# A two-layer attention trunk: four modulation rows, the first loads, the first norm, the rotary tables and the steps of the last two heads are put elsewhere

## The chip, the cores and the metric

The kernel runs on one core of a Trainium2 chip. The metric is the device time of one execution in microseconds; lower is better. A core has a matrix engine (TensorE, PE in the profile), a vector engine (VectorE, DVE), a scalar engine (ScalarE, ACT), a small general engine (GpSimd, POOL) and a queue engine (SyncE, SP) that issues nearly all of this kernel's DMAs. Each engine runs its own instructions in a fixed order; between engines there are semaphores. TensorE writes its sums to PSUM banks, from which VectorE and ScalarE read.

## The reference

One sequence of 256 tokens and 2048 features passes through two layers. Layer 0 mixes tokens by NSA attention (16 query heads, 4 key and value heads, a compressed, a selected and a window branch), layer 1 by differential attention (8 heads, each with two softmaxes). Each mixer is followed by an MLP of 8192 hidden features with squared ReLU. Every sub-layer is modulated by shift, scale and gate vectors that are computed from one vector c. All data are float32.

```python
mod_all = einsum('bd,lde->lbe', silu(c), ada_w) + ada_b[:, None, :]   # ada_w (2, 2048, 6*2048)
for i in range(2):
    sh1, sc1, g1, sh2, sc2, g2 = jnp.split(mod_all[i][:, None, :], 6, axis=-1)
    h = rms_norm(x, attn_norm_g[i]) * (1.0 + sc1) + sh1
    y = nsa_mixer(h, positions, ...) if i == 0 else diff_mixer(h, positions, ...)
    x = x + g1 * y
    h = rms_norm(x, mlp_norm_g[i]) * (1.0 + sc2) + sh2
    x = x + g2 * (jnp.square(jax.nn.relu(h @ w1)) @ w2)
# diff_mixer, per head: a = softmax(q0 k0) - lam * softmax(q1 k1); o = rms_norm(a @ v) ; y = o @ w_out
```

## The kernel before

x stays in SBUF with features on partitions: `xT` is 128 x 16 x 256, 16 blocks (kt) of 128 features by 256 tokens. Weights arrive as `raw` tiles of 128 x 1024 (512 KB). For most matrix products ScalarE rounds such a tile to `wH`, VectorE forms `wL = raw - wH` (`split`, L254 on), and TensorE does three products for every one of the reference: wH by the rounded activations, wH by their rest, wL by the rounded ones. There are 721 such tiles.

**The modulation.** `ada_w` is read as 192 rows of 128 x 2048 (1 MB each). A row is multiplied by silu(c) and summed on VectorE by one `scalar_tensor_tensor` (stt). The 32 rows of layer 0's first scale and shift are called `adarow` and belong to the first stage, two per block (`lead_ada`, L720). The other 160, `adaraw`, come from a queue (`ada_step`): each tile of weights adds a rate to a credit, and each full credit takes a row. The rates are the constants RA, RB, RC for NSA, DR for the projections of layer 1, MR0, MR1 and CR for the MLPs. Four rows of this queue (40 to 43, `PE_ROWS`) are stored otherwise and summed by TensorE: `pe_row` makes 16 small matmuls into `adps` for each, `pe_add` four more into `ade`.

**The first stage.** It begins with the first norm (L431 to L436): ScalarE squares each block of xT, TensorE sums the squares over partitions with a matrix of ones into `nps`, and `rstd_of` takes the root in VectorE and ScalarE steps named `nst`, `ny`, `nu`. Then come 16 blocks kt. Each needs its two rows, one weight tile for the compressed branch (16 matmuls `psc`) and one for values or keys (8 matmuls `psv` or `psk`). h of a block is made by VectorE (`nt`), ScalarE (`h`, twice) and VectorE (`h`, the rest). Blocks 0 to 7 use psc and psv, then psk is done for them, and blocks 8 to 15 use psc and psk. `trig` and `rope_table` (L440 on) make sines, cosines and the rotary tables from the positions; the code calls them in block kt = 3. The compression weights `cwk`, `cwv` follow the window projection `psw`.

**The heads of layer 1.** Four groups g of two heads. Per group `dk`, `dq` and `dv` are projections in four steps u. Work for the heads waits in a list `pend`: normalising and turning keys and queries (`norm`, `both`, `flip`; transposes `tps` of `qr`), then for each of two heads `scores` (`dsc`), `turn` (`aps`), `pv` (`dops`, then `on`, a normalised copy) and `back` (`otp`, then `od`). `pop()` takes the first entry of the list at each step u of a later projection; what is left at the end of dv of group 3 is taken in `dwo`, the output projection, one entry per step.

**What sets the order.** A scheduler of the tile framework orders the instructions of every engine by priority; the text of the program gives the priority, `high_priority` moves a row ahead, and `issue_after(ins)` places an instruction behind `ins` on that engine without making it wait. Tile pools limit how far ahead loads go: 5 buffers for raw, 3 for `adaraw`, 8 in the pool of `adarow` of which h holds four, 3 each for wH and wL, and in PSUM banks 4 for projections, 1 in `sd` and 3 in `sc`.

Of the kernel before, what the change touches and what calls it, by code (L numbers as in the profile page):

```python
# [19 lines left out]
P = 128  # L20
# [16 lines left out]
RA, RB, RC = 1.34, (1.25, 1.5, 1.5, 1.5), (2.0, 0.9)  # L37

PE_ROWS = range(40, 44)
DR = 0.4  # L40
MR0 = 0.72
# [36 lines left out]
def emit(ctx, tc, nc, a):  # L78
# [45 lines left out]
    for q in range(4):  # L124
        nc.sync.dma_start(xT[:, q * 4:(q + 1) * 4, :], a["xT"][:, q * 4:(q + 1) * 4, :])
# [28 lines left out]
    last_load = [None]  # L154

# [5 lines left out]


    e4 = cst.tile([P, 1], F32, name="e4")
    V.tensor_reduce(out=e4, in_=ident[:, 0:P:32], axis=mybir.AxisListType.X, op=ALU.add)
    pe_rows, pe_open, pe_sums = [], [], []

    def on_pe(l, vec, kt):
        return l == 0 and ada_q.index((l, vec, kt)) in PE_ROWS

    def pe_row(l, vec, kt, r):  # L170
        w = r.rearrange("p (k n) -> p k n", k=KT)
        if not pe_open:
            pe_open.append(sc("adps"))
        ps = pe_open[0]
        j = len(pe_open) - 1
# [4 lines left out]
        pe_open.append(kt)  # L180
        if j == 3:
            four = sm.tile([P, 4, P], F32, tag="qr", bufs=QRB, name="four")
            act(four, ps.rearrange("p (j n) -> p j n", j=4))
            pe_sums.append((l, vec, kt - 3, four))
            pe_open.clear()

    def pe_add():
        while pe_sums:
            l, vec, kt, four = pe_sums.pop(0)
            ps = sd("ade")  # L190
            for j in range(4):
                TE.matmul(ps[:, j:j + 1], four[:, j], e4, start=j == 0, stop=j == 3)
            e = vec * KT + kt
            tt(mod[:, l, vec, kt:kt + 4], ps[:, :4], bT[:, l, e:e + 4], ALU.add)

    def pe_flush(keep):
        if len(pe_rows) > keep:
            pe_add()
            for _ in range(2):
                pe_row(*pe_rows.pop(0))  # L200

    def ada_tile(l, vec, kt):
# [3 lines left out]
        if on_pe(l, vec, kt):  # L206
            pe_rows.append((l, vec, kt, r))
            pe_flush(2)
            return
# [4 lines left out]
    def ada_row(vec, kt):  # L214
        r = actp.tile([P, D], F32, tag="act", name="adarow")
        nc.sync.dma_start(r, a["adaT"][0, vec * KT + kt])
        acc = acc_tile(0, vec)[:, kt:kt + 1]
        stt(r, r, 1.0, cbc, ALU.mult, ALU.mult, accum_out=acc)
        return acc

    def ada_vec(l, vec):
        e = vec * KT
        cuts = [0] + [kt for kt in range(1, KT) if on_pe(l, vec, kt) != on_pe(l, vec, kt - 1)] + [KT]
        for lo, hi in zip(cuts, cuts[1:]):
            if not on_pe(l, vec, lo):
                tt(mod[:, l, vec, lo:hi], acc_tile(l, vec)[:, lo:hi], bT[:, l, e + lo:e + hi], ALU.add)
# [21 lines left out]
    def ada_until(l, vec):  # L248
# [3 lines left out]
        if any(p[:2] == (l, vec) for p in pe_rows + pe_sums):  # L252
            while pe_rows:
                pe_flush(0)  # L254
            pe_add()
# [982 lines left out]
```

## Time and profile before

| | us |
|---|---|
| three timed runs | 2356.14, 2358.07, 2363.26 |
| their median | 2358.07 |
| the profiled execution | 2358.31 |
| its span in the trace | 2356.3 |
| TensorE busy | 2323.1 (99%) |
| VectorE busy | 1734.8 (74%) |
| ScalarE busy | 1183.5 (50%) |

The profile shows one execution. A row of a timeline gives the start, the time from the first instruction's start to the last one's end, and, in brackets, how long the engine had been idle before and what released it. Matmuls are pipelined, so the lengths of two rows overlap; the distance between starts is what a row costs. PEclk is the clock that was granted to TensorE: 1.00 is 2.4 GHz, 0.5 is 1.2 GHz, and a value between them for a stretch is a mean over time at either. In 40 equal slices of the span TensorE stands at 9 tenths busy or more in all but the first, the granted clock at 9 or more in all but the first, and the share of the DMA engines is 9 tenths in the first four.

### The profile page before, as it was taken

The numbers are of one execution on the slowest core, as the hardware profiler recorded it, in microseconds if no ns is written. First come the engines' busy times: TensorE is split into PE (matmuls) and PEld (weight loads), VectorE is DVE, ScalarE is ACT, GpSimd is POOL, SyncE is SP. The second block draws the span as 40 slices with busy tenths as digits, with TensorE's granted clock in tenths as the row PEclk, the third lists the DMA queues.
The fourth block names the chain that finished last, engine by engine and source line by source line (L and its number), as shares of the span: only waits on it lengthen the run. The fifth ranks groups of instructions, "written<-read, shape, count | busy, mean of one in ns | idle before, by whom it ended". The sixth has DMA issues, their size and how long they took to land.

```text
span 2356.3 us, 34910 instructions
## 1 busy us (share of the span) xinstructions
PE 2323.1 (99%) x13465; PEld 1998.3 (85%) x13465; DVE 1734.8 (74%) x2418; ACT 1183.5 (50%) x2055; POOL 44.8 (2%) x41
## 2 busy tenths in 40 slices
PE   7999999999999999999999999999999999999999
PEld 5767778998888888888898888799988888888888
DVE  6867999699888888888888777766755555555555
ACT  3223788455345345445556556555643543543553
POOL 0000000000000000000000100000000000000000
PEclk8999999999999999999999999999999999999999
DMA  9999777779888888888867666645555555555554
GB/s 358 404 371 354 292 306 264 267 279 371 337 308 324 329 310 327 319 308 333 306 226 247 222 238 233 210 159 170 194 188 187 183 189 187 187 188 187 187 194 147
DMA packets 139846, 612.19 MB, mean 260 GB/s; under 512 B 15648, under 2 KB 16288, under 8 KB 114080
## 3 DMA queue, kind: packets, MB, share of 16 engines
q1 hardware_dynamic: 139536, 609.71, 71.6%
q8 instruction: 105, 1.72, 0.3%
q14 instruction: 61, 0.50, 0.1%
q10 hardware_dynamic: 144, 0.26, 0.0%
HBM read 607.81 MB, written 2.10 MB: 259 GB/s over the span
## 4 chain that ended last, share of the span: by engine, by line
PE 71%; DVE 1%; DMA 1%; issue 1%; ACT 0%; POOL 0%; POOLq 0%; SPq 0%; DVEq 0%
PE m L301 36%; PE m L308 17%; PE dwo L293 1%; PE dwo L294 1%; PE dwo L295 1%; PE m L304 1%; PE dk L285 1%; PE dk L286 1%; PE dk L287 1%; PE dv L287 1%; PE dv L286 1%; PE dv L285 1%; PE dq L285 1%; PE dq L286 1%; PE dq L287 1%; DMA adaraw<-adaT 1%
## 5 line engine op out<-in xcount | busy, mean ns | idle before, releaser
L97 ACT ACTIVATE wH<-raw 128x1024 fp32r<-128x1024 f32 x721 | 762.3, 1059 | 895.7 <-PE m L301 655.2
L262 DVE TENSOR_TENSOR wL<-raw,wH 128x1024 fp32r<-128x1024 f32 x721 | 877.5, 1222 | 451.0 <-ACT wH L97 449.5
L301 PE MATMUL m<-hd,wH 128*128 128x512 f32 x2048 | 710.4, 396 | 0.0
L301 PE MATMUL m<-hn,wH 128*128 128x512 f32 x1792 | 624.7, 397 | 0.0
L308 PE MATMUL m<-hd,wL 128*128 128x256 f32 x1920 | 534.5, 280 | 4.5 <-DVE wL L262 4.5
L308 PE MATMUL m<-hn,wL 128*128 128x256 f32 x1680 | 470.7, 281 | 0.0
L301 PEld LDWEIGHTS m<-hd,wH 128*128 128x128 f32 x2048 | 376.1, 188 | 80.2
L301 PEld LDWEIGHTS m<-hn,wH 128*128 128x128 f32 x1792 | 329.7, 188 | 71.0
L103 DVE SCALAR_TENSOR_TENSOR adaraw<-adaraw,cbc 128x2048 f32<-128x2048 f32 x156 | 356.2, 2285 | 25.0 <-DMA adaraw<-adaT 23.2
L308 PEld LDWEIGHTS m<-hd,wL 128*128 128x128 f32 x1920 | 361.4, 189 | 12.7 <-DVE wL L262 6.1
L308 PEld LDWEIGHTS m<-hn,wL 128*128 128x128 f32 x1680 | 317.2, 189 | 5.9 <-DVE wL L262 0.2
L103 DVE SCALAR_TENSOR_TENSOR xT<-m,mod,xT 128x256 f32<-128x256 f32 x256 | 108.8, 478 | 38.8 <-PE m L301 38.7
L103 DVE SCALAR_TENSOR_TENSOR adarow<-adarow,cbc 128x2048 f32<-128x2048 f32 x32 | 73.2, 2286 | 8.7 <-DMA adarow<-adaT 4.4
L293 PE MATMUL dwo<-od,wH 128*128 128x256 f32 x256 | 73.5, 290 | 0.6 <-ACT od L97 0.6
L295 PE MATMUL nwo<-o,wL 128*128 128x256 f32 x256 | 73.3, 286 | 0.0
L295 PE MATMUL dwo<-od,wL 128*128 128x256 f32 x256 | 73.0, 286 | 0.0
L293 PE MATMUL nwo<-o,wH 128*128 128x256 f32 x256 | 73.0, 285 | 0.0
L294 PE MATMUL dwo<-od,wH 128*128 128x256 f32 x256 | 72.9, 285 | 0.0
L294 PE MATMUL nwo<-o,wH 128*128 128x256 f32 x256 | 72.8, 284 | 0.0
L293 PE MATMUL m_z<-z,wH 128*128 128x258 f32 x256 | 72.7, 284 | 0.0
L735 PEld LDWEIGHTS psc<-h,raw 128*128 128x128 f32 x256 | 51.7, 205 | 24.5 <-ACT h L97 10.3
L294 PE MATMUL m_z<-z,wH 128*128 128x258 f32 x256 | 72.3, 283 | 0.0
(317 smaller groups left out, 3242.8 us busy)
## 6 DMA issues: line engine op xcount, KB each, us to landing
raw<-w SPq DMA_DIRECT2D x512, 512.0 KB, 4.3
adaraw<-adaT SPq DMA_DIRECT2D x160, 1024.0 KB, 7.0
raw<-di SPq DMA_DIRECT2D x96, 512.0 KB, 4.1
adarow<-adaT SPq DMA_DIRECT2D x32, 1024.0 KB, 12.4
raw<-ws SPq DMA_DIRECT2D x48, 512.0 KB, 10.5
raw<-wi SPq DMA_DIRECT2D x32, 512.0 KB, 6.4
raw<-nwo SPq DMA_DIRECT2D x32, 512.0 KB, 5.0
raw<-dwo SPq DMA_DIRECT2D x32, 512.0 KB, 3.5
```

Of the source, the lines that this page charges most:

```text
L97: return S.activation(out=out, in_=in_, func=func, **kw)
L103: V.scalar_tensor_tensor(out, in0, scalar, in1, op0=op0, op1=op1, **kw)
L262: last_split[1] = V.tensor_tensor(out=L[:, :n], in0=raw[:, :n], in1=H[:, :n].bitcast(F32), op=ALU.subtract).ins
L285: TE.matmul(ps, xh, H[:, off:off + n], start=first, stop=False)
L286: TE.matmul(ps, xh, L[:, off:off + n], start=False, stop=False)
L287: TE.matmul(ps, xl, H[:, off:off + n], start=False, stop=last)
L293: TE.matmul(ps, H[:, off:off + m], xh, start=first, stop=False)
L294: TE.matmul(ps, H[:, off:off + m], xl, start=False, stop=False)
L295: TE.matmul(ps, L[:, off:off + m], xh, start=False, stop=last)
L301: big = lambda stop: TE.matmul(ps.rearrange("p (a t) -> p a t", a=2), H[:, off:off + P], at, start=first, stop=stop)
L308: TE.matmul(ps[:, :T], L[:, off:off + P], at[:, 0], start=False, stop=False)
L735: TE.matmul(ps_c[i][n // 2][:, (n % 2) * T:(n % 2 + 1) * T], w[:, i * 512 + n * P:i * 512 + (n + 1) * P], full, start=f and n % 2 == 0, st ...
```

## The change

- The four rows on TensorE go: `pe_row`, `pe_add` and `pe_flush` are removed, and all 160 rows are summed by VectorE.
- The rates of the row queue become RC (2.2, 0.8), DR 0.45, MR0 0.65.
- The first norm squares four blocks per instruction: ScalarE squares 128 x 1024, VectorE another 128 x 1024, VectorE adds the two, and TensorE sums 4 blocks for each half instead of 8.
- The loads of the first stage get a fixed order behind the last load of xT; the weight tiles of a block come behind its rows, `posi`, `rowb` and `mk` behind a weight tile.
- `trig`, the tables and the casts of masks come behind the rows of the fourth block.
- Three of the four value weights of the compression (`cwv`) are loaded in blocks 13 to 15, ahead of `cwk`.
- In dv of group 3 two entries of `pend` are taken at each of the four steps, in an order in which the two heads go side by side.

```diff
-RA, RB, RC = 1.34, (1.25, 1.5, 1.5, 1.5), (2.0, 0.9)
-
-PE_ROWS = range(40, 44)
-DR = 0.4
-MR0 = 0.72
+RA, RB, RC = 1.34, (1.25, 1.5, 1.5, 1.5), (2.2, 0.8)
+DR = 0.45
+MR0 = 0.65
...
-    def pe_row(l, vec, kt, r):
...
-        for k in range(KT):
-            i = k % 4
-            TE.matmul(ps[i * 32:(i + 1) * 32, j * P:(j + 1) * P], cs[:, k:k + 1].to_broadcast([P, 32]), w[:, k],
-                      start=j == 0 and k < 4, stop=j == 3 and k >= KT - 4, tile_position=(0, i * 32))
...
     def ada_row(vec, kt):
         r = actp.tile([P, D], F32, tag="act", name="adarow")
-        nc.sync.dma_start(r, a["adaT"][0, vec * KT + kt])
+        with tc.issue_after(last_load[0]) if vec * KT + kt in FIRST else nullcontext():
+            last_row[0] = nc.sync.dma_start(r, a["adaT"][0, vec * KT + kt]).ins
         acc = acc_tile(0, vec)[:, kt:kt + 1]
-        stt(r, r, 1.0, cbc, ALU.mult, ALU.mult, accum_out=acc)
+        last_row[1] = V.scalar_tensor_tensor(r, r, 1.0, cbc, op0=ALU.mult, op1=ALU.mult, accum_out=acc).ins
         return acc
+
+    last_row = [None, None]
+    FIRST = [v * KT + kt for v in range(2) for kt in range(KT // 2)]
...
-    for kt in range(KT):
-        sq = sm.tile([P, T], F32, tag="nsq", name="nsq0", bufs=4)
-        act(sq, xT[:, kt, :], AF.Square)
-        TE.matmul(nps[:, :T], ones, sq, start=(kt == 0), stop=(kt == KT - 1))
+    for i in range(2):
+        two = [p.tile([P, 1024], F32R, tag=tag, name="sq0").bitcast(F32) for p, tag in ((whp, "wh"), (wlp, "wl"))]
+        for j in range(2):
+            x4 = xT[:, (i * 2 + j) * 4:(i * 2 + j + 1) * 4, :].rearrange("p k t -> p (k t)")
+            if j:
+                tt(two[j], x4, x4, ALU.mult)
+            else:
+                act(two[j], x4, AF.Square)
+        tt(two[0], two[0], two[1], ALU.add)
+        for k in range(4):
+            TE.matmul(nps[:, :T], ones, two[0][:, k * T:(k + 1) * T], start=i + k == 0, stop=i * 4 + k == 7)
...
+    def pop_two(u):
+        pend.pop(0)()
+        pend.pop(1 if u == 0 else 0)()
...
-        wc = wcols(kt, 0)
-        wv = wcols(kt, 1)
+        with tc.issue_after(last_row[0]):
+            wc = wcols(kt, 0)
+            wv = wcols(kt, 1)
...
         if kt == 3:
-            trig()
-            tab_ks = rope_table(ROW_KS, 0, 2, "tab_ks")
...
+            with tc.issue_after(last_row[1]):
+                trig()
+                tab_ks = rope_table(ROW_KS, 0, 2, "tab_ks")
...
+        if kt >= KT - 3:
+            cwv.append(values_weights(kt - KT + 3))
...
-            ps = xs_group(f"dv{g}_", lambda u: a["di"][g * 3, u], h1, DR, lambda u: pop(g == 3 and u < 2))
+            ps = xs_group(f"dv{g}_", lambda u: a["di"][g * 3, u], h1, DR, lambda u: pop_two(u) if g == 3 else pop())
```

Three places of the resulting order are shown. The first is VectorE in the first stage; `trb` is the angle of `trig`, `adarow` a row of a block, and `h_202`, `h_203` hold h of blocks 0 to 3 and 4 to 7 (`h_170`, `h_171` after). Before, from the end of block 0's h to the second row of block 1:

```order
21 L100 TENSOR_TENSOR h_202<-h_237,h_202 128x256
22 L445 CAST trb<-posi 128x3
23 L107 TENSOR_SCALAR trb<-co,trb 128x64 x3
24 L109 TENSOR_SCALAR trb<-trb 128x192
25 L107 TENSOR_SCALAR trb<-trb 128x192
26 L109 TENSOR_SCALAR trb<-trb 128x192 x2
27 L100 TENSOR_TENSOR trb<-trb 128x192
28 L103 SCALAR_TENSOR_TENSOR trb<-trb 128x192 x6
29 L109 TENSOR_SCALAR trb<-trb 128x192
30 L103 SCALAR_TENSOR_TENSOR adarow,adaacc<-adarow,cbc 128x2048
31 L107 TENSOR_SCALAR trs<-trs 128x3x64
32 L103 SCALAR_TENSOR_TENSOR Amod<-adaacc,b_211,smallT 128x1
```

After, from the second row of block 3 to the first row of block 4; block 1 now has only its rows and its own steps on VectorE:

```order
42 L400 CAST trb<-posi 128x3
43 L736 CAST maskb<-mk 128x288
44 L98 TENSOR_TENSOR mod<-adaacc,smallT 128x1
45 L105 TENSOR_SCALAR trb<-co,trb 128x64 x3
46 L737 CAST identb<-co 128x128
47 L107 TENSOR_SCALAR trb<-trb 128x192
48 L105 TENSOR_SCALAR trb<-trb 128x192
49 L98 TENSOR_TENSOR h_170<-h_299,h_170 128x256
50 L107 TENSOR_SCALAR trb<-trb 128x192 x2
51 L98 TENSOR_TENSOR trb<-trb 128x192
52 L101 SCALAR_TENSOR_TENSOR trb<-trb 128x192 x5
53 L170 SCALAR_TENSOR_TENSOR adarow,adaacc<-adarow,cbc 128x2048
```

The angles and tables have moved from between blocks 0 and 1 to between blocks 3 and 4.

The second is ScalarE at the end of the heads, where `dwo` runs on TensorE. Before, with `on` the normalised result of a head and `od` its turned copy:

```order
815 L97 ACTIVATE wH<-raw 128x1024 x6
816 L97 ACTIVATE on,dss<-dops 128x256 x2
817 L97 ACTIVATE on<-dops,dss 128x256 x2
818 L97 ACTIVATE wH<-raw 128x1024 x2
819 L97 ACTIVATE on,dss<-dops 128x256 x2
820 L97 ACTIVATE on<-dops,dss 128x256 x2
821 L97 ACTIVATE od_13952<-otp,subg 128x256
822 L97 ACTIVATE z_1_0_14196<-mod 128x4x2
823 L97 ACTIVATE od_13952<-otp,subg 128x256 x3
824 L97 ACTIVATE wH<-raw 128x1024
```

After:

```order
807 L95 ACTIVATE wH<-raw 128x1024 x6
808 L95 ACTIVATE on,dss<-dops 128x256 x2
809 L95 ACTIVATE on<-dops,dss 128x256 x2
810 L95 ACTIVATE wH<-raw 128x1024 x2
811 L95 ACTIVATE on,dss<-dops 128x256 x2
812 L95 ACTIVATE on<-dops,dss 128x256 x2
813 L95 ACTIVATE wH<-raw 128x1024 x2
814 L95 ACTIVATE od_13832<-otp,subg 128x256
815 L95 ACTIVATE z_1_0_14143<-mod 128x4x2
816 L95 ACTIVATE od_13832<-otp,subg 128x256
817 L95 ACTIVATE wH<-raw 128x1024 x2
818 L95 ACTIVATE od_13832<-otp,subg 128x256 x2
```

Behind the second head's `on` now stand two weight tiles before the first `od`, and before there were none; the four `od` of the last pair of heads all stand behind them.

The third is VectorE in the first MLP, where `hd` is the hidden layer and `xT` takes up the result. Before:

```order
622 L100 TENSOR_TENSOR hd_0_3_5002<-sq,hd_0_3_5002 128x2x256
623 L262 TENSOR_TENSOR wL<-raw,wH 128x1024
624 L100 TENSOR_TENSOR hd_0_3_5002<-sq,hd_0_3_5002 128x2x256
625 L262 TENSOR_TENSOR wL<-raw,wH 128x1024
626 L103 SCALAR_TENSOR_TENSOR adaraw,adaacc<-adaraw,cbc 128x2048 x2
627 L262 TENSOR_TENSOR wL<-raw,wH 128x1024 x2
628 L103 SCALAR_TENSOR_TENSOR adaraw,adaacc<-adaraw,cbc 128x2048
629 L262 TENSOR_TENSOR wL<-raw,wH 128x1024 x2
```

After, at the same weight tiles (the 117th and on):

```order
628 L210 TENSOR_TENSOR wL<-raw,wH 128x1024
629 L101 SCALAR_TENSOR_TENSOR adaraw,adaacc<-adaraw,cbc 128x2048
630 L98 TENSOR_TENSOR hd_0_3_4900<-sq,hd_0_3_4900 128x2x256 x2
631 L210 TENSOR_TENSOR wL<-raw,wH 128x1024 x2
632 L101 SCALAR_TENSOR_TENSOR adaraw,adaacc<-adaraw,cbc 128x2048
633 L210 TENSOR_TENSOR wL<-raw,wH 128x1024 x2
634 L101 SCALAR_TENSOR_TENSOR adaraw,adaacc<-adaraw,cbc 128x2048
635 L210 TENSOR_TENSOR wL<-raw,wH 128x1024 x2
```

Two rows in a run have become single rows with two weight tiles between them.

## Rows read from the trace of the kernel before

**Rows 1.** The page, part 1: span, busy time and instructions of each engine

```profile
span 2356.3 us, 34910 instructions
...
PE 2323.1 (99%) x13465; PEld 1998.3 (85%) x13465; DVE 1734.8 (74%) x2418; ACT 1183.5 (50%) x2055; POOL 44.8 (2%) x41
```

**Rows 2.** Waits of PE, whole span: line, releaser, total, times, longest (us)

```profile
PE psc L735 <- ACT h L97: 7.1, 2, 4.3
...
PE m L308 <- DVE wL L262: 4.5, 3, 1.7
PE otp L1073 <- ACT on L97: 3.4, 2, 2.8
PE tps L532 <- DVE qr L100: 3.0, 2, 2.0
```

**Rows 3.** The page, part 5: costliest groups; mean ns behind the busy time

```profile
L262 DVE TENSOR_TENSOR wL<-raw,wH 128x1024 fp32r<-128x1024 f32 x721 | 877.5, 1222 | 451.0 <-ACT wH L97 449.5
...
L103 DVE SCALAR_TENSOR_TENSOR adaraw<-adaraw,cbc 128x2048 f32<-128x2048 f32 x156 | 356.2, 2285 | 25.0 <-DMA adaraw<-adaT 23.2
```

**Rows 4.** Timeline of PE around 450 and 484 us: start, length, instructions

```profile
449.49 1.95 PE L178 MATMUL adps<-adaraw,cs 128*32 128x128 f32 x64
451.38 0.39 PE L293 MATMUL nwo<-o,wH 128*128 128x256 f32 x1
...
483.73 1.05 PE L192 MATMUL ade<-e,four 128*128 128x1 f32 x8
484.65 0.37 PE L293 MATMUL m_z<-z,wH 128*128 128x258 f32 x1
```

**Rows 5.** Busy time per stretch (x instructions), PEclk, DMA share, GB/s

```profile
400.00:485.00 85.00, 84.92 (x790) 83.07 (x789) 62.39 (x109) 47.34 (x91) 0.00 (x0) 1.00 0.71 260
500.00:540.00 40.00, 40.00 (x310) 38.60 (x309) 39.96 (x66) 28.82 (x54) 0.00 (x0) 1.00 0.71 258
...
1480.00:1520.00 40.00, 36.41 (x167) 29.08 (x166) 26.85 (x37) 20.19 (x46) 3.37 (x4) 1.00 0.60 212
1560.00:1580.00 20.00, 16.59 (x110) 15.85 (x110) 9.83 (x19) 9.68 (x21) 0.69 (x1) 0.83 0.25 82
```

**Rows 6.** Timeline of DVE, first MLP

```profile
584.45 2.29 DVE L103 SCALAR_TENSOR_TENSOR adaraw<-adaraw,cbc 128x2048 f32<-128x2048 f32 x1
...
586.66 2.29 DVE L103 SCALAR_TENSOR_TENSOR adaraw<-adaraw,cbc 128x2048 f32<-128x2048 f32 x1
```

**Rows 7.** Timeline of PE: idle time before an instruction, and its releaser

```profile
590.15 0.74 PE L308 MATMUL m<-hd,wL 128*128 128x256 f32 x4 [1.08 <-DVE wL L262]
...
1498.66 0.63 PE L532 MATMUL tps<-co,qr 128*128 128x128 f32 x4 [2.00 <-DVE qr L100]
...
1565.68 0.66 PE L1073 MATMUL otp<-co,on 128*128 128x128 f32 x4 [2.84 <-ACT on L97]
1566.90 1.22 PE L293 MATMUL dwo<-od,wH 128*128 128x256 f32 x4 [0.56 <-ACT od L97]
```

**Rows 8.** Timeline of PE in the first stage

```profile
22.18 5.98 PE L735 MATMUL psc<-h,raw 128*128 128x256 f32 x16 [4.28 <-ACT h L97]
...
34.41 6.69 PE L735 MATMUL psc<-h,raw 128*128 128x256 f32 x16 [2.82 <-ACT h L97]
...
51.25 3.62 PE L735 MATMUL psc<-h,raw 128*128 128x256 f32 x16
...
58.14 3.62 PE L735 MATMUL psc<-h,raw 128*128 128x256 f32 x16
```

**Rows 9.** Timeline of DVE in the first stage

```profile
22.60 0.43 DVE L100 TENSOR_TENSOR h<-h,h 128x256 fp32r<-128x256 f32 x1 [1.02 <-ACT h L97]
...
27.74 2.28 DVE L103 SCALAR_TENSOR_TENSOR adarow<-adarow,cbc 128x2048 f32<-128x2048 f32 x1
...
34.87 0.42 DVE L100 TENSOR_TENSOR h<-h,h 128x256 fp32r<-128x256 f32 x1
...
50.04 2.29 DVE L103 SCALAR_TENSOR_TENSOR adarow<-adarow,cbc 128x2048 f32<-128x2048 f32 x1 [0.97 <-DMA adarow<-adaT]
```

More of the change, by code (lines that the diff above doesn't have):

```diff
@@ L1 @@
 import math
-from contextlib import ExitStack, contextmanager
+from contextlib import ExitStack, contextmanager, nullcontext
 import numpy as np
@@ L159, in acc_tile @@
         return adaacc[l, vec]
[L163 to L168, printed above, removed]
-    def pe_row(l, vec, kt, r):
[L171 to L175, printed above, removed]
-        for k in range(KT):
-            i = k % 4
-            TE.matmul(ps[i * 32:(i + 1) * 32, j * P:(j + 1) * P], cs[:, k:k + 1].to_broadcast([P, 32]), w[:, k],
-                      start=j == 0 and k < 4, stop=j == 3 and k >= KT - 4, tile_position=(0, i * 32))
[L180 to L200, printed above, removed]
     def ada_tile(l, vec, kt):
@@ L251, in ada_until @@
             ada_step(1.0)
[L252 to L255, printed above, removed]
     def split(raw, n=1024):
@@ L730, in full_of, with values_weights @@
         return modulate_full(h, kt, rstd, Amod[:, 0, 0, kt:kt + 1], mod[:, 0, 0, kt:kt + 1])
+    def values_weights(lu):
+        wv = adap.tile([P, 8, 256], F32, tag="ada", name="cwv")
+        with tc.issue_after(last_load[0]):
+            nc.sync.dma_start(wv.rearrange("p l f -> p (l f)"), a["cw1"][1, lu])
+        return wv
+    cwv = []
     def c_mm(w, full, f, la):
@@ L756, in emit @@
         if kt == 1:
-            nc.sync.dma_start(posi, a["posT"])
-            nc.sync.dma_start(rowb, a["rows"][:, :ROW_LAM * DH].to_broadcast([P, ROW_LAM * DH]))
             mk = wkp.tile([P, 288], F32, tag="qT", name="mk", bufs=1)
-            nc.sync.dma_start(mk, a["consts"][:, CO_M0:CO_N])
+            with tc.issue_after(last_load[0]):
+                nc.sync.dma_start(posi, a["posT"])
+                nc.sync.dma_start(rowb, a["rows"][:, :ROW_LAM * DH].to_broadcast([P, ROW_LAM * DH]))
+                nc.sync.dma_start(mk, a["consts"][:, CO_M0:CO_N])
         if kt == 3:
-            trig()
-            tab_ks = rope_table(ROW_KS, 0, 2, "tab_ks")
-            tab_kw = rope_table(ROW_KW, 0, 2, "tab_kw")
-            V.tensor_copy(maskb, mk)
-            V.tensor_copy(identb, ident)
-            w2c = wkp.tile([P, 2, 2, DH], F32, tag="qT", name="w2c", bufs=1)
-            nc.sync.dma_start(w2c, a["cw2"])
+            with tc.issue_after(last_row[1]):
+                trig()
+                tab_ks = rope_table(ROW_KS, 0, 2, "tab_ks")
+                tab_kw = rope_table(ROW_KW, 0, 2, "tab_kw")
+                V.tensor_copy(maskb, mk)
+                V.tensor_copy(identb, ident)
+                w2c = wkp.tile([P, 2, 2, DH], F32, tag="qT", name="w2c", bufs=1)
+                nc.sync.dma_start(w2c, a["cw2"])
     for i in range(2):
@@ L825, in cmp_part @@
         nc.sync.dma_start(wk.rearrange("p l f -> p (l f)"), a["cw1"][0, lu])
-        wv = adap.tile([P, 8, 256], F32, tag="ada", name="cwv")
-        nc.sync.dma_start(wv.rearrange("p l f -> p (l f)"), a["cw1"][1, lu])
+        wv = cwv.pop(0) if cwv else values_weights(lu)
         for j in range(8):
@@ L1193 @@
     ins["adaT"] = c_(ada_w.transpose(0, 2, 1).reshape(DEPTH, NVEC, P, D))
-    for n in PE_ROWS:
-        e = (2, 4, 3, 5)[n // KT] * KT + n % KT
-        ins["adaT"][0, e] = ada_w[0][:, e * P:(e + 1) * P].reshape(KT, P, P).transpose(1, 0, 2).reshape(P, D)
     wi = nsa_w_in[0]
```

12 lines of the change are left out of this document (2 added, 10 removed).

## The prediction

> **What bounds the kernel now.** I read the page's busy times first. TensorE is busy 2323.1 of 2356.3 us [rows 1], so 33.2 us at most can be won by taking waits away; more has to come from its own work. The waits of TensorE come next [rows 2]: four kinds make 18.0 of the 33.2 us. They lie in three places, and the change touches all three: the first stage (7.1 us for h), single weight tiles `wL` (4.5), and the heads of layer 1 (3.4 for `on`, 3.0 for `qr`). Last I read the stretches [rows 5]: VectorE is full in 500 to 540 us (39.96 of 40), yet TensorE has no idle time there; a row too early in a run, as at 590 us, does cost 1.08 [rows 7]. The granted clock is 1.00 in all of them but the last, 1560 to 1580, where it is 0.83, a mix of the levels 2.4 and 1.2 GHz. So a time is set here by TensorE's work, by a late VectorE or ScalarE result at few places, and by the clock after such a wait.
>
> **The four rows on TensorE.** One group of 64 small matmuls costs 1.89 us (from 449.49 to the next work at 451.38), and there are two; the eight matmuls of `ade` cost 0.92 (483.73 to 484.65) and about 0.2 in front of them [rows 4]. All of it is in TensorE's own line: 2 x 1.89 + 1.1 = **-4.9 us**. VectorE gets four rows more, 4 x 2.285 = 9.1 us [rows 3], and by the rates six rows more (43 to 49) stand before the end of the NSA output projection: 6 x 2.285 = 13.7 us. In 400 to 485 us VectorE is idle 85 - 62.4 = 22.6 us [rows 5], which covers them. Not all of that is free when it is wanted: the last NSA heads' steps then stand behind a row. Bounds: nothing, and a row's rest with a wL behind, 1.5; I take +0.7. Without the cover the price is up to 9.1, which is a rival below.
>
> **The first MLP.** TensorE waits 1.08 us at 590.15 because the wL it needs stands behind two rows in a run, at 584.45 and 586.66 [rows 6, 7]. In the new order single rows alternate there with two weight tiles, since rows are ahead by four. Of the three waits for wL (4.5 us, the longest 1.7 [rows 2]) this one goes. A second of 1.7 near 1147 us stands behind a row and a burst of xT steps; the lower rate moves the row away, and it goes too, nearly. The third, in front of which only xT steps stand, stays. So 1.08 + 1.7 = 2.8, of which I take **-2.7**; bounds 0 (another tile becomes late; a run of two rows now stands at the 113th tile) and -4. That the rates leave as many rows to layer 1 costs nothing in the second half: VectorE has room (in 1480 to 1520 us it is busy 26.8 of 40 [rows 5]).
>
> **The paired heads.** Today the two heads of the last group follow each other and their ends have no work beside them. The list of waits gives 3.0 (qr) and 3.4 (on), and 0.56 for od at 1566.90 [rows 2, 7]. After the 2.84 us at 1565.68 the granted clock falls: a mean of 0.83 over 20 us [rows 5] is 3.4 us of time lost at 1.2 GHz. Together 10.4; about 1.5 more is lost as the array runs empty and fills at each of five waits (an estimate of 0.3 each), so some 11.9 us are there to win. The new order takes two steps per weight pair in dv, so `norm` and `flip` of the queries come where dv still runs, and after the last `on` ScalarE does two weight tiles, while TensorE has 48 matmuls of dwo in front of the first `otp`; at 84.9 / 790 = 0.107 us each [rows 5] that is 5.2 us for a chain that needed 2.84 more than it had. What is late next: two heads' scores need four score banks in a row where three exist, and the fourth waits until ScalarE has done one exponential behind a weight tile: its `wL` sibling takes 1.22 us [rows 3], so I take 1.3; and 0.3 for the single `sd` bank. Sum -11.9 + 1.6 = **-10.3**. Bounds: -12 if nothing new waits; -6 if both heads' softmax pushes three weight tiles late by 1.22 us each and the idle time at the end is only halved.
>
> **The first stage.** Block 0 starts at 22.18 now, block 1 after 2.82 us of waiting at 34.41 [rows 8]. The wide squares leave ScalarE and TensorE earlier, but block 0's two rows must still land and pass VectorE, so I leave 22.18 as it is (bounds 0.7 either way). Then the angles: today they stand between block 0's h (22.60) and block 1's second row (27.74, the first of that block on VectorE), 4.8 us, and the tables follow until 34.87 [rows 9]. Without them blocks 1 to 3 come earlier; the 2.82 us and the second stretch at 1.2 GHz go (6.69 against 3.62 us for the same 16 matmuls, 3.07 [rows 8]). Together that is 5.9 us. But it isn't kept. The rows of a block come by DMA, and block 4's first row already waits for its DMA, 0.97 us at 50.04 [rows 9]. The angles now stand around exactly this block's rows: some 5 us of them in front of the first row, the rest and the tables, 2.5 us, in front of h. Block 4 then starts at about 50.04 + two rows of 2.2 + 2.5 for angles and tables + 1 for its own small steps = 57.9, against 58.14 [rows 8], and TensorE, done with block 3 5.9 us earlier than now, at about 52.2, waits some 5.7 us in front of it. A wait of 2.82 was followed by the lower clock [rows 8], so this one will be as well: block 4 loses up to 3.07 that it doesn't lose today, of which I count 2 from its later start to the keys of blocks 0 to 7. The loads that wait for freed buffers behind it shift, but three of today's short waits for them go. **+0.9** remains; bounds -4 (the angles fit into VectorE's wait for block 4's row) and +3 (all of the lower clock is kept, and the shift too). The masks and `w2c` moved with it cost VectorE 0.5 us inside the same wait.
>
> TensorE's clock is where a page speaks against this move. The row shows that 16 matmuls of a block take 6.69 us behind an idle time of 2.82, and 3.62 at full clock [rows 8]; and that a wait of 2.00 us at 1498.66 was followed by none of it (granted clock 1.00 in 1480 to 1520 [rows 5, 7]). The Trainium skill, "TensorE: Matmul & The Clock Gate", section "Why this matters for your kernels", advises against idle gaps between bursts of matmuls, since the engine goes back to half clock after them. By that rule one gap of 5.7 us before block 4 is no better than the present gap before block 1; without the rule the sum would be some 2 us lower.
>
> **Window keys and compression weights.** In front of the first wL of `psw` VectorE now copies all of `kcT`. That stage has no wait in the list today; at worst two weight tiles are late by 1.22 us each [rows 3]. I take +1.3 (0 to 2.5). The three early `cwv` loads fall into a stretch with DMA to spare and cost nothing; should they push weight tiles late, one 1 MB tile each, the +3 above holds this too.
>
> **The sum.** -4.9 + 0.7 - 2.7 - 10.3 + 0.9 + 1.3 = -15.0 us against the profiled execution of 2358.31, which is 0.24 above the median of the three runs: **2343.3 us**.
>
> **Rivals.**
> - *The heads give less back.* The burst of two heads on ScalarE and VectorE delays wL, and the banks of `sc` and `sd` become the wait. For it: two entries per step in a stretch where ScalarE and VectorE also make weight tiles. Against it: VectorE is a third idle there. The gain falls from 10.3 to about 4: 2349.6.
> - *VectorE's extra rows are on the path.* For it: VectorE is full in 500 to 540 us, right behind. Against it: TensorE didn't wait there. Uncovered, four rows cost 9.1: about 2352.
> - *The first stage is bound by DMA alone* and the angles fit into VectorE's waits. For it: VectorE waits 0.97 us for a row at 50.04. Against it: 7 us of angles don't fit into one such wait. Both the 2.82 and a lower clock go, -5: about 2337.5.
> - *Slower: the lower clock stays on.* The mechanism is TensorE's clock from block 4 on. A block takes 6.89 us (51.25 to 58.14 [rows 8]), its eleven others as much. If each is followed by a wait for rows that are late because of the angles, TensorE falls to 1.2 GHz again and again, at 3.07 us a time: eight times cost 25, about 2368. It decides from 22 us above the forecast on, that is from the seventh time. For it: the clock fell after two waits in this stage [rows 8]. Against it: at 51.25 and 58.14, with VectorE as full, the same 16 matmuls take 3.62 us [rows 8].
> - *It doesn't do what it says:* the fixed order of first loads moves no bytes earlier, as the queue carried them nearly in this order; this is already in the sum with nothing.
>
> **How the numbers follow.** About 0.3%, 7 us, is what a measurement of this kernel tells from no change, so faster means below 2351.0. My forecast 0.70 (2338 to 2349), less from the heads 0.12, the rows on the path 0.08, the DMA-bound stage 0.06, the clock 0.04. Faster: 0.70, 0.06 and of the heads' rival 0.10, together 0.86. Within 0.3%: its other 0.02 and the rows on the path, 0.08, together 0.10. Slower: the clock, 0.04. The range of 8 in 10 is 2336 to 2351: the unknown bounds of stage one and heads do not all fall on one side.
>
> **What would show it.** Right: no `adps`; no wait of `otp` for `on`, and clock 1.00 where `dwo` runs; waits for wL below 2.5 us in all; a single wait for h of about 5 to 6 us before the fifth psc block, with 16 matmuls above 6 us behind it. Wrong: waits of dsc for ScalarE above 2 us; nwo or m waiting for wL between 440 and 560 us; a clock below 0.9 in 60 to 120 us; block 1 still behind h for over 2 us.

## The result, and the profile after

| | before | changed |
|---|---|---|
| median of the runs, us | 2360.98 | 2346.59 |
| profiled execution, us | 2358.31 | 2347.46 |
| its span, us | 2356.3 | 2345.3 |

The changed kernel takes 2346.59 us (2345.07 to 2347.46 in five runs); the ratio to before is 0.9945 with a 95% interval of 0.9929 to 0.9960. One of the five runs of the kernel before took 2832.83 us and is not in the ratio; the median of the other four is 2359.5. So the gain is about 13 us by the timed runs and 11.0 between the two traces. The forecast was 2343.3, with a range of 2336 to 2351.

Page of the changed kernel, part 1, in answer to [rows 1]:

```profile
span 2345.3 us, 34602 instructions
...
PE 2314.0 (99%) x13313; PEld 1988.6 (85%) x13313; DVE 1745.7 (74%) x2427; ACT 1177.0 (50%) x2040; POOL 46.2 (2%) x41
```

TensorE has 152 instructions fewer (13465 to 13313): 128 `adps`, 8 `ade` and 16 of the first norm. These float32 matmuls stand in the trace as two records each: the program has 64 for `adps`, 4 for `ade` and 8 fewer in the norm. The list of TensorE's waits, in answer to [rows 2]:

```profile
PE psc L703 <- ACT h L95: 10.0, 2, 5.2
...
PE m L256 <- DVE wL L210: 3.3, 3, 1.7
PE dv L234 <- DVE wL L210: 1.9, 1, 1.9
...
PE otp L1045 <- DVE od L101: 0.4, 1, 0.4
```

`otp` no longer waits for `on`, nor `tps` for `qr`. The first stage's wait is longer than before, 10.0 against 7.1, three waits of m for wL remain, and one is new: dv for wL, 1.9.

How far the changed kernel's TensorE is ahead is read by the starts of the same matmuls in the two traces. The first `m_z` of the first MLP, behind the NSA output projection; first of before, then of the changed kernel:

```profile
482.06 0.39 PE L293 MATMUL m_z<-z,wH 128*128 128x258 f32 x1
```

```profile
478.01 0.28 PE L241 MATMUL m_z<-z,wH 128*128 128x258 f32 x1
```

Read in this way over the whole trace, in us (negative is ahead; `dvz` is dv of group 0):

| place | lag | what lies between |
|---|---|---|
| first psk | -0.49 | blocks 0 to 7 |
| first q | -0.24 | blocks 8 to 15, window keys, compression |
| first nwo | -0.32 | NSA heads |
| first m_z | -4.05 | both groups of `adps` gone |
| first m of the first MLP, behind its m_z | -5.74 | `ade` gone |
| first dvz | -5.47 | the first MLP |
| first dk of group 2 | -2.0 | the new wait in dv of group 1 |
| last dq | -1.75 | |
| last dwo | -11.57 | the paired heads |
| last matmul | -10.97 | the second MLP |

The first stage, in answer to [rows 8], TensorE's timeline of the changed kernel:

```profile
21.23 6.01 PE L703 MATMUL psc<-h,raw 128*128 128x256 f32 x16 [5.20 <-ACT h L95]
...
30.51 3.62 PE L703 MATMUL psc<-h,raw 128*128 128x256 f32 x16
...
56.11 5.41 PE L703 MATMUL psc<-h,raw 128*128 128x256 f32 x16 [4.77 <-ACT h L95]
...
64.78 3.62 PE L703 MATMUL psc<-h,raw 128*128 128x256 f32 x16
```

The wait in front of block 1 has become one of 4.77 us in front of block 4, counted from 0, and the 16 matmuls behind it take 5.41 instead of 3.62. VectorE, in answer to [rows 9]: block 4's first row no longer waits for its DMA, and starts 2.5 us earlier.

```profile
47.53 2.29 DVE L170 SCALAR_TENSOR_TENSOR adarow<-adarow,cbc 128x2048 f32<-128x2048 f32 x1
```

The stretches of the heads, in answer to the last two of [rows 5]; columns as there:

```profile
1480.00:1520.00 40.00, 39.48 (x195) 31.93 (x194) 29.41 (x43) 23.61 (x54) 4.25 (x4) 1.00 0.66 235
...
1560.00:1580.00 20.00, 20.00 (x169) 20.00 (x168) 18.54 (x33) 13.54 (x26) 0.00 (x0) 1.00 0.84 300
```

TensorE is busy 39.48 of 40 us in the first stretch, where it was 36.41, and the granted clock of the second is 1.00, where it was 0.83.

The new wait, TensorE and then VectorE of the changed kernel:

```profile
1343.19 0.60 PE L234 MATMUL dv<-wL,hn 128*128 128x512 f32 x1 [1.90 <-DVE wL L210]
```

```profile
1336.31 2.29 DVE L101 SCALAR_TENSOR_TENSOR adaraw<-adaraw,cbc 128x2048 f32<-128x2048 f32 x1 [2.47 <-DMA adaraw<-adaT]
1338.52 0.08 DVE L101 DVE_READ_ACCUMULATOR adaraw<-adaraw,cbc 128x1 f32 x1
1338.52 0.17 DVE L105 TENSOR_SCALAR qs<-qss 128x4 f32<-128x4 f32 x1
```

A row of the queue stands in front of the steps of group 1's queries (`qs`, `qr`), and VectorE waits 2.47 us for its DMA. Then wL is late, and the granted clock falls behind the 1.90 us. The stretch of the next 4 us:

```profile
1343.00:1347.00 4.00, 3.81 (x10) 2.98 (x11) 3.68 (x6) 0.00 (x0) 0.00 (x0) 0.57 0.50 146
```

Ten matmuls there; the 5 us behind it hold 27 at a clock of 1.00. Wait and clock together are the 3.7 us by which the lag falls.

### The profile page after: what moved, and what is told of

The parts are those of the page before. It is cut to its first block, busy times and chain, and to the rows that moved or that the text cites. A ratio compares the mean times of both kernels' runs of the same rounds, so it can differ in the third digit from the quotient of the medians.

```text
span 2345.3 us, 34602 instructions
## 1 busy us (share of the span) xinstructions
PE 2314.0 (99%) x13313; PEld 1988.6 (85%) x13313; DVE 1745.7 (74%) x2427; ACT 1177.0 (50%) x2040; POOL 46.2 (2%) x41
## 4 chain that ended last, share of the span: by engine, by line
PE 72%; DVE 1%; DMA 1%; ACT 0%; issue 0%; POOL 0%; SPq 0%
PE m L249 36%; PE m L256 17%; PE dwo L241 1%; PE dwo L243 1%; PE dwo L242 1%; PE m L252 1%; PE dq L234 1%; PE dq L235 1%; PE dq L233 1%; PE dk L233 1%; PE dk L234 1%; PE dk L235 1%; PE m_z L242 1%; PE m_z L241 1%; PE m_z L243 1%; PE dv L234 1%
## 5 line engine op out<-in xcount | busy, mean ns | idle before, releaser
L101 DVE SCALAR_TENSOR_TENSOR adaraw<-adaraw,cbc 128x2048 f32<-128x2048 f32 x160 | 365.4, 2285 | 33.3 <-DMA adaraw<-adaT 32.8
L703 PE MATMUL psc<-h,raw 128*128 128x256 f32 x256 | 62.3, 399 | 11.0 <-ACT h L95 10.0
```

The lines of the kernel that those rows point to most:

```text
L101: V.scalar_tensor_tensor(out, in0, scalar, in1, op0=op0, op1=op1, **kw)
L703: TE.matmul(ps_c[i][n // 2][:, (n % 2) * T:(n % 2 + 1) * T], w[:, i * 512 + n * P:i * 512 + (n + 1) * P], full, start=f and n % 2 == 0, st ...
```

## The experiments

Each was timed in five rounds (the rows alone with eleven runs) beside the kernel before, on the same chip. Ratios are to before, with 95% intervals; times are medians in us. Three chips were used: one for the paired heads, the old heads, DR 0.4 and the angles behind the eighth block (before took 2360.88 there), one for the rows, the old rates, the changed kernel beside them and "no row in dq" (2360.39), one for the last four (2361.28). Kernels of different chips are better compared by their ratios.

| kernel | time | ratio |
|---|---|---|
| changed | 2346.59 | 0.9945 (0.9929 to 0.9960) |
| changed, beside the others | 2345.5 | 0.9939 (0.9925 to 0.9952) |
| before with paired heads only | 2350.55 | 0.9955 (0.9943 to 0.9968) |
| changed with the old heads | 2351.69 | 0.9959 (0.9946 to 0.9971) |
| before with all rows on VectorE only | 2357.57 | 0.9983 (0.9975 to 0.9992) |
| changed, old rates | 2348.68 | 0.9952 (0.9939 to 0.9964) |
| changed, DR 0.4 | 2351.74 | 0.9959 (0.9947 to 0.9972) |
| changed, angles behind the eighth block | 2344.76 | 0.9929 (0.9915 to 0.9943) |
| the same, no row in dq of group 1 | 2346.12 | 0.9940 (0.9928 to 0.9953) |
| changed, angles in front of the third block | 2344.99 | 0.9936 (0.9922 to 0.9951) |
| changed, rows a step later | 2342.75 | 0.9923 (0.9910 to 0.9936) |
| changed, rows behind the newest wL | 2341.15 | 0.9918 (0.9905 to 0.9931) |
| that, and angles behind the eighth block | 2338.45 | 0.9907 (0.9892 to 0.9921) |

**The paired heads.** The kernel before, with the new steps alone:

```diff
-lambda u: pop(g == 3 and u < 2))
+lambda u: pop_two(u) if g == 3 else pop())
```

> The kernel before, with nothing but the paired steps in dv of group 3. If the pairing itself gives what the traces show between the end of dq and the end of dwo (a lag that goes from -1.75 to -11.6 us), this kernel is 9 to 11 us faster than before (ratio 0.9955 to 0.996), its trace has no wait of otp for `on`, no wait of tps for `qr`, and no stretch at 1.2 GHz near 1566 us. If the gain comes from the new rates, which change where rows stand on VectorE in the same stretch, it is within 3 us of before and the waits remain.

It took 2350.55, 10.3 us below before. Between the last dq and the last dwo its lag went from -0.87 to -10.28, so 9.4 us come from this place; the clock in the last stretch is 1.00:

```profile
1560.00:1580.00 20.00, 20.00 (x168) 19.80 (x167) 18.13 (x34) 13.38 (x27) 0.00 (x0) 1.00 0.54 181
```

The reverse edit in the changed kernel:

```diff
-lambda u: pop_two(u) if g == 3 else pop())
+lambda u: pop(g == 3 and u < 2))
```

> The changed kernel with the single steps of before in dv of group 3, and all else changed. If the pairing is the cause, it loses 9 to 11 us of the 11 to 13 and stands about 2 us below the kernel before (ratio 0.998 to 1.0); the wait of otp for `on` of 2.8 us and the lower clock behind it are back. If the rates are the cause, it keeps most of the gain (ratio near 0.996).

It took 2351.69, 5 to 6 us more than the changed kernel by the medians and 3 to 5 by the ratios, whose intervals overlap; not 9 to 11. TensorE's timeline shows the old end:

```profile
1558.15 0.66 PE L1045 MATMUL otp<-co,on 128*128 128x128 f32 x4 [2.78 <-ACT on L95]
1559.37 0.74 PE L241 MATMUL dwo<-od,wH 128*128 128x256 f32 x4 [0.56 <-ACT od L95]
```

Against the second trace of the changed kernel the lag rises by 6.8 us over layer 1's attention. The waits of `tps` for the query steps (3.0 before) are 1.0 here, although the heads are the old ones: in the kernel before a row stands on VectorE just in front of these steps, and here the last one ended 7 us earlier. What such a row costs changes from trace to trace. It is shown in the kernel before and then, at the same place, in the kernel with the rows alone (below), which has the old heads and the old rates:

```profile
1491.66 2.29 DVE L103 SCALAR_TENSOR_TENSOR adaraw<-adaraw,cbc 128x2048 f32<-128x2048 f32 x1 [2.29 <-DMA adaraw<-adaT]
```

```profile
1489.44 2.29 DVE L103 SCALAR_TENSOR_TENSOR adaraw<-adaraw,cbc 128x2048 f32<-128x2048 f32 x1 [0.46 <-DMA adaraw<-adaT]
```

With 2.29 us of waiting for the row's load the waits of `tps` for `qr` are 3.0, with 0.46 they are 1.2. So some 1.8 us of what the heads win against this one trace of before is a late row, which another place of the rows takes away as well, and the expected loss of 9 to 11 was too high. In both directions the wait of `otp` for `on`, and the lower clock behind it, come and go with the pairing: it is the cause of the larger part.

**The rows on VectorE.** The kernel before, with one edit:

```diff
-PE_ROWS = range(40, 44)
+PE_ROWS = range(0)
```

> The kernel before with all 160 rows on VectorE and nothing else changed (rates, heads, first stage as before). If the removed TensorE work is worth its time there and VectorE's slack covers the rows, TensorE is 5 to 5.5 us ahead of before at the first matmul of the MLP (two steps of 1.9 near 450 and 480 us, 1.2 near 484) and the ratio is 0.9975 to 0.998. If VectorE's extra rows are on the path, the lag at that point is smaller than 3 us, or is lost again by 600 us in longer waits for wL.

The lag went from +3.3 at the first nwo to -2.5 at the first m: 5.8 us, a little more than expected, and nothing came back in 485 to 600 us. The whole gained only 2.8 us by the medians, 4.0 by the ratio (2 to 6). In its trace the first stage was 3.3 us late with the same program there, and 4.2 us were lost between dvz and the start of dwo, in waits of `tps` for `vtile` and `krs` and of `otp` for `on`, one of them of 2.48 us with the lower clock behind it (a clock of 0.62 in the next 4 us). Whether these come from the rows isn't shown; with the heads alone, where no row was moved, 1.4 us are lost at the first of these places too.

```profile
PE psc L735 <- ACT h L97: 10.5, 3, 4.7
PE otp L1073 <- ACT on L97: 5.3, 2, 2.8
...
PE tps L532 <- DVE vtile L100: 1.2, 1, 1.2
PE tps L532 <- DVE krs L109: 0.8, 1, 0.8
```

**The rates.** All three as before, in the changed kernel:

```diff
-(2.2, 0.8)
-DR = 0.45
-MR0 = 0.65
+(2.0, 0.9)
+DR = 0.4
+MR0 = 0.72
```

> The changed kernel with the three rates of before (RC, DR, MR0). Theory: the rates themselves gain nothing in the first MLP (the waits for wL move but stay 4 to 5 us in all) and cost up to 3.7 us in layer 1, where a row whose DMA lands late stands in front of the query steps of group 1; with the old rates VectorE's order there is that of before, so this kernel is 1 to 4 us faster than the changed one, run beside it. Rival: the rates are worth 2.7 us in the first MLP, as predicted; then this kernel is 2 to 3 us slower.

2348.68 against 2345.5 beside it: not faster, as my theory had it, but 3 us slower with intervals that overlap, and not for the rival's reason. Its waits of m for wL are 4.0 against 3.3 and 3.5 in the two traces of the changed kernel, but over the first MLP its lag changes by 0.2, theirs by 0.3 and 0.7: the rates win nothing there. Its trace has one new wait in layer 1, with a clock of 0.61 in the 4 us behind it; it costs 3.6 us, about as much as the changed kernel's in its first trace:

```profile
1272.54 1.09 PE L487 MATMUL tps<-co,vtile 128*128 128x128 f32 x4 [2.94 <-DVE krs L107]
```

With only DR put back:

```diff
-DR = 0.45
+DR = 0.4
```

> The changed kernel with the row rate of layer 1's projections back at 0.4. Theory: the new wait of dv for wL near 1343 us (1.9 us, and 0.43 us instead of 0.23 for each of the next ten or so matmuls at half clock) comes from one row that the rate 0.45 puts in front of the steps of the queries in dv of group 1. Then the wait goes and the kernel is 3 to 4 us faster than the changed one (about 2343). Rival: the row's late DMA is what counts (VectorE waited 2.5 us for it), and another tile waits for it instead; then the time stays within 1 us of the changed kernel.

My theory fell: 2351.74, slower by 5 to 6 us by the medians and 3 to 5 by the ratios, whose intervals overlap. The row did move, and other tiles waited: dv 2.1, dq 1.4, dwo 1.0. VectorE's idle time in front of `adaraw` was 51.0 us in this trace, against 33.3 in the changed kernel's. So it is not that one place in the order; the suspicion is rows that stand in front of whatever comes next while their DMA is still under way.

**Chance in the changed kernel.** The changed kernel again, with no edit:

> The changed kernel once more, beside the others and with a second trace. It is the measure for the three others of this call. If the wait near 1343 us depends on when a DMA lands, it differs by over 1 us between the two traces, with the same order on every engine; and the start of psk differs by 1 us or more as well. If it depends on the order alone, both traces show it at 1.9 us.

The same program, second trace, VectorE and TensorE at the place of the new wait:

```profile
1333.38 2.29 DVE L101 SCALAR_TENSOR_TENSOR adaraw<-adaraw,cbc 128x2048 f32<-128x2048 f32 x1 [0.90 <-DMA adaraw<-adaT]
```

```profile
1340.27 0.50 PE L234 MATMUL dv<-wL,hn 128*128 128x512 f32 x1 [0.32 <-DVE wL L210]
```

The row's load took 8.1 us from issue (1328.26) to VectorE's start in the first trace and 6.5 (1326.92) in the second; the wait is 1.90 in one and 0.32 in the other, with the same order. Two kernels below have that order at this place too. Over the four traces (changed again, angles behind the eighth block, changed, angles in front of the third) VectorE waits 0.90, 1.59, 2.47 and 2.73 us for the row's load, and dv waits 0.32, 1.01, 1.90 and 2.16 for wL: 0.57 to 0.58 less each time. The late load is the cause of this wait. Psk starts 1.6 us earlier, since block 4 waited 3.46 and kept its clock:

```profile
56.13 3.72 PE L703 MATMUL psc<-h,raw 128*128 128x256 f32 x16 [3.46 <-ACT h L95]
```

So the two spans, 2345.3 and 2340.7, differ by two such events, and a few microseconds of one trace are no property of the kernel.

**The place of the angles.** Behind the rows of the eighth block:

```diff
-        if kt == 3:
+        if kt == 7:
             with tc.issue_after(last_row[1]):
```

> The changed kernel with angles and tables behind the rows of the eighth block instead of the fourth. If TensorE's wait of 4.8 us before block 5 and the 1.8 us at half clock behind it are lost time, the kernel is 5 to 6.5 us faster than the changed one. If the first 160 us are bound by DMA, the wait goes but comes back as short waits for rows and weight tiles in blocks 5 to 14, and the gain at the start of psw is at most 1.5 us.

The wait before block 4 is gone, and the blocks come 7.5 us apart instead of 6.9:

```profile
52.65 3.72 PE L703 MATMUL psc<-h,raw 128*128 128x256 f32 x16
...
60.08 3.72 PE L703 MATMUL psc<-h,raw 128*128 128x256 f32 x16 [0.27 <-ACT h L95]
...
67.60 3.72 PE L703 MATMUL psc<-h,raw 128*128 128x256 f32 x16 [0.37 <-ACT h L95]
...
75.23 3.72 PE L703 MATMUL psc<-h,raw 128*128 128x256 f32 x16 [0.48 <-ACT h L95]
```

Psk starts at 81.8 and psw at 161.8, 0.6 us before the second trace of the changed kernel and 2.5 before the first. By time it is within 1 to 2 us of the changed kernel (2.4 to 3.8 by the ratios, with intervals that overlap), not resolved. Near their old place:

```diff
-            with tc.issue_after(last_row[1]):
+            with nullcontext():
                 trig()
```

> The changed kernel with angles and tables between the second and the third block, near their old place. The two traces of the changed kernel start psk at 85.0 and 83.4 us, the kernel with the angles behind block 8 at 81.8, and by psw the three are at 164.3, 162.4 and 161.8. If the first stage is bound by DMA from about 110 us on, this kernel too reaches psw at 162 to 164.5 and its time is within 2 us of the changed one (2344 to 2348). If the place of the angles decides, an idle time before block 3 with a stretch at 1.2 GHz costs 3 us or more at psw.

It waits 2.96 us before block 2, without a fall of the clock, and reaches psw at 162.1; 2344.99, the same as the changed kernel. Four traces (angles behind the eighth block, behind the fourth twice, in front of the third) lie within 2.5 us at psw, and the three in which the clock did not fall a second time within 0.6.

All fourteen traces say more, as most of them share their first stage, with the same order on TensorE, VectorE and ScalarE, with another. In the seven in which the clock does not fall again after block 0, psw starts at 161.8 to 163.0 us, whether the angles stand behind the eighth block (three traces), behind the fourth (two), in front of the third, or where they were before (162.7, heads only). With one such fall it is 164.3 to 164.8 (six traces, among them before and changed), with two 168.1 (rows alone). So the first stage of the kernel before takes 162.7, 164.8 or 168.1 with one program, that of the changed kernel 162.4 to 164.7. A wait of 3.0 to 3.5 us in front of a block costs at most 1 us at psw if the clock holds, which agrees with a stage that something else bounds, such as DMA; no run changed the bytes. A fall costs some 2 us, and they aren't made up. With the angles behind the eighth block no block waits over 0.6 us for h behind block 0, and the clock did not fall again in any of the three traces; behind the fourth it did in five of seven.

The order of the first loads, the wide squares of the first norm and the early `cwv` were not taken back one by one, so what each is worth isn't shown.

**Rows that don't stop VectorE.** First, with the angles behind the eighth block, no row from dq of group 1 and twice the rate in its dv:

```diff
-dq: xs_group(..., h1, DR, ...)
+dq: xs_group(..., h1, 0.0 if g == 1 else DR, ...)
-dv: xs_group(..., h1, DR, ...)
+dv: xs_group(..., h1, 2 * DR if g == 1 else DR, ...)
```

> The kernel with the angles behind block 8, with one more edit: no rows are taken from the queue in dq of group 1, and twice the rate in dv of group 1, so that no row stands directly in front of the query steps. If the late row is the cause, the wait of dv for wL there (1.0 to 1.9 us in three traces) and the half clock behind it go, and the kernel is 1 to 3 us faster than with the angles alone (about 2342). If rows wait for their DMA wherever they stand, another weight tile waits as long and the time stays at 2344 to 2346.

2346.12: no gain. dv still waits 1.4 in three places and dq 0.7, and VectorE waits 40.4 us for rows. Moving one row moves the wait. Then all rows, in the changed kernel, behind the newest wL of their step:

```diff
-        with tc.high_priority(offset=-AOFF):
+        with tc.issue_after(last_split[1]), tc.high_priority(offset=-AOFF):
             stt(r, r, 1.0, cbc, ...)
```

> The changed kernel, with every row of the queue summed behind the newest wL of its own step. As with the step later, by half: idle time before `adaraw` between 15 and 33 us, the wait near 1341 us gone, as the row no longer stands in front of the query steps; 0 to 2 us faster than the changed kernel.

2341.15, more than expected. The groups of VectorE's rows, the changed kernel and then this one (busy, mean ns, idle before):

```profile
L101 DVE SCALAR_TENSOR_TENSOR adaraw<-adaraw,cbc 128x2048 f32<-128x2048 f32 x160 | 365.4, 2285 | 33.3 <-DMA adaraw<-adaT 32.8
```

```profile
L101 DVE SCALAR_TENSOR_TENSOR adaraw<-adaraw,cbc 128x2048 f32<-128x2048 f32 x160 | 365.4, 2285 | 4.0 <-DMA adaraw<-adaT 4.0
```

The same 365.4 us of work, and 4.0 instead of 33.3 of waiting for a DMA. The edit also takes the row's own 2.29 us from in front of a weight tile, and this experiment doesn't part the two; at the place near 1340 the four traces above do. Between its trace and the changed kernel's first, the lag improves by 2.2 us over the first MLP and by 3.7 in dv of group 1. Its list of TensorE's waits has no dv or dq for wL, and m for wL is down to

```profile
PE m L256 <- DVE wL L210: 2.3, 2, 1.7
```

With the sum one step later still, beside the edit above:

```diff
+        ada_ahead.append((l, vec, kt, r))
+        if len(ada_ahead) > 1:
+            ada_sum(*ada_ahead.pop(0))
+
+    def ada_sum(l, vec, kt, r):
         with tc.issue_after(last_split[1]), tc.high_priority(offset=-AOFF):
             stt(r, r, 1.0, cbc, ...)
```

> The changed kernel, with every row of the queue summed one step after its load and behind the newest wL. If rows whose DMA lands late are what delays wL in layer 1, VectorE's idle time before `adaraw` falls from 33 to 36 us to under 15, no wait of dv or dq for wL is left, and the kernel is 0 to 3 us faster than the changed one, with less spread between its runs. If the waits come from where VectorE's work stands at all, others appear and the time stays or grows by up to 4.

2342.75; 1.6 us of idle time before `adaraw` and no wait of m for wL over 0.3 us. It isn't faster than the last; its trace has two waits of `tps` for late VectorE steps (0.9 us each) and 0.6 of `ptps` that the last does not have.

Last, both edits, `kt == 7` for the angles and `issue_after(last_split[1])` for the rows:

```diff
-        if kt == 3:
+        if kt == 7:
...
-        with tc.high_priority(offset=-AOFF):
+        with tc.issue_after(last_split[1]), tc.high_priority(offset=-AOFF):
```

> The changed kernel with the angles behind block 8 and every row behind the newest wL of its step. If both are local and real, it is the fastest: 2341 to 2344. If the first stage is bound by DMA and the rows' wait is chance, it is the same as the changed kernel within 2 us (2344 to 2347).

2338.45 (2337.65 to 2339.25), ratio 0.9907 (0.9892 to 0.9921): it beats both kernels, and the changed one by 7 to 8 us (7 to 9 by the ratios), with intervals that don't meet. It is 2.7 us below the kernel with the rows behind the newest wL, beside which it ran and from which only the place of the angles parts it; all five of its runs are below all five of the other, and in the traces psw starts 2.7 us earlier (161.9 against 164.7), where the clock fell once less. Its page:

```profile
span 2336.4 us, 34613 instructions
...
PE 2311.3 (99%) x13313; PEld 1988.1 (85%) x13313; DVE 1746.7 (75%) x2427; ACT 1177.6 (50%) x2040; POOL 42.1 (2%) x41
```

## Why the prediction was right, and where it wasn't

*Time.* 2346.59 lies within the range and on the side that was forecast, 3.3 us above it. By the traces the gain is 11.0 of the 15.0 forecast. The two large terms hold. That the sum came as near is luck in part: against the forecast stand the first MLP (3.0), a wait that was not foreseen (3.7) and 0.6 lost in the second MLP, for it the first stage with the window keys (2.4) and the four rows (1.2). In the second trace of the same kernel the gain is 15.6, and each term is measured against one trace of the kernel before.

*The four rows.* Forecast -4.9 + 0.7; the lag changes by 5.4 from the first nwo to the first m, and by 5.8 with this edit alone. VectorE's slack covers them; the +0.7 for late NSA heads is not seen, and what goes with `ade` was 1.7 (from the first m_z to the first m), not 1.1.

*The first MLP.* Forecast -2.7, measured +0.3. This step failed: I took the position of rows in VectorE's order for the cause and reckoned that better positions end the waits. The wait at 590 us went as said, but by the lag 0.9 us are lost near 578, where two wL stand behind a row and two steps of `hd`: the bounds had named another tile that becomes late. The wait near 1147 only moved:

```profile
1166.52 0.74 PE L256 MATMUL m<-hd,wL 128*128 128x256 f32 x4 [1.28 <-DVE wL L210]
```

In front of it on VectorE stand a row from 1157.99 on and the burst of xT steps behind it, as at the old place. With the rows behind the newest wL this wait is gone. So these two are rows in front of a weight tile, wherever the rates put them. The third wait is still 1.73, as the prediction said, and no row makes it: wL stands behind xT steps, for which VectorE itself waits for TensorE.

```profile
592.68 0.48 DVE L101 SCALAR_TENSOR_TENSOR xT<-m,mod,xT 128x256 f32<-128x256 f32 x1 [1.74 <-PE m L249]
```

It stays with the rows behind the newest wL and goes only with the rows a step later, where two wL stand in front of the same xT steps.

*The paired heads.* Forecast -10.3, measured -9.8 and -9.9 in the two traces, and -9.4 with this edit alone. Each part is as described: no wait for `qr` or `on`, a clock of 1.00. Some 1.8 us of the 3.0 for `qr` were a late row in this trace of before, not the order of the heads. The 0.3 us by which a wait costs more than its idle time has no row: by the starts of the matmuls around the waits of 1.08, 2.00 and 2.84 it is 0.16 (at 590.15 the start comes 1.47 behind the last one, of which 1.08 are idle and 0.23 the usual distance). So 11.2 rather than 11.9 were there to win, and new waits took about 1.4 of it; 1.6 was forecast.

*The first stage and the window keys.* Forecast +0.9 and +1.3, measured -0.6 by psw and +0.3 in it, in the first trace; -2.4 and +0.3 in the second. The mechanism was right in place and size: a single wait in front of block 4 of 4.77 (5.7 forecast), block 4 at 56.1 (57.9), the clock falling behind it. Together the two terms were too high by 2.4 to 4.3 us: block 4's row came 2.5 us earlier than before, so the wait was shorter, and in the second trace the clock did not fall. How +0.9 is added up the prediction doesn't show, and the three short waits of psc for weight tiles that were to go are still there in the first trace (1.0 us, 1.2 before). But these are differences from one trace: the first stage of before itself starts psw 2.1 us earlier (heads only) and 3.3 later (rows alone) in two others. Whether the change of the first stage gains or loses anything is not resolved.

*Not foreseen.* The new wait in dv of group 1, which with the clock behind it costs 3.7 us in one trace and is 0.3 in another. The prediction asked what stands behind a row on VectorE, but took every row's load as landed; [rows 3] showed the 23.2 us that VectorE waits for `adaraw`'s DMA already, and I let it stand as idle time.

*The rivals.* The heads gave nearly all they should. VectorE's rows were not on the path as a sum, but were as late loads. The first stage bound by DMA is the rival that came nearest, but not as it was told: the angles don't fit into VectorE's waits (4.77 in front of block 4), and a fall of the clock still costs 2 us at psw; where it holds, psw starts at 161.8 to 163.0 in all orders of the angles. The clock that stays low didn't come: from 64.78 on the blocks run at 3.62.

*The signs.* Of those named for being right, `adps` and the wait of `otp` for `on` are gone, the clock is 1.00 where `dwo` runs, and one wait for h, of 4.77, stands in front of the fifth block. Two did not come: the waits of m for wL are 3.3, not below 2.5, and the 16 matmuls behind the wait take 5.41, not above 6. None of those for being wrong came.

## What to carry to other kernels

Idle time in front of a filler instruction on an engine with slack isn't free where an in-order queue puts urgent work behind it: read what releases the filler, and place it behind the urgent work rather than at the moment at which its data should have landed. Two independent chains of small steps that run side by side hide each other's latencies where one after the other they show all of them. And before a term of two or three microseconds is believed, look at two traces of the same program.

## What the runs showed of the hardware

The granted clock did not follow the length of the wait alone. It fell to 1.2 GHz behind waits of TensorE of 1.90 us (changed, 1343), 2.19 (rows alone, 66), 2.82 (before, 34), 2.94 (rows behind wL, 57), 3.89 (rows a step later, 56) and 4.77 (changed, 56), and stayed at 2.4 GHz behind 2.00 (before, 1498), 2.16 (angles in front of the third block, 1342), 2.96 (the same, 42), 3.01 (heads only, 35), 3.22 (old heads, 56) and 3.46 (changed again, 56). Three places had both: that in front of block 4, behind 4.77 and 3.46, that in front of block 1 of the kernel before, behind 2.82 and 3.01, and dv of group 1, behind 1.90 and 2.16, with the longer wait the one that kept the clock at the last two.

A 1 MB load of a row took 8.1 and 6.5 us from issue to use at the same place of the same program, which is enough to move a wait of VectorE from 0.90 to 2.47 us.
